# Five of seven down products of a ConvFFN from scaled pairs of float16 instead of pairs of fp32r

## The chip, the core and the metric

The kernel runs on one core of a Trainium2 chip. The metric is the device time of one execution in microseconds (us), the median of several runs. A core has TensorE (PE in the profile, with its weight loads as PEld), VectorE (DVE), ScalarE (ACT), GpSimd (POOL) and SyncE (SP), which here only starts DMAs. Each engine works through its own queue in order, and waits on semaphores of the others.

## The reference

One decoder layer: attention and a gated short convolution side by side, then a feed-forward part with a causal depthwise convolution over time. All of it is float32. What the change touches is the last part:

```python
h2 = rmsnorm(x, norm2_g) * (1 + sc2) + sh2
u = causal_dwconv(h2 @ w_up, ffn_conv_w)          # 3 taps
u_gate, u_val = jnp.split(u, 2, axis=-1)
y = (silu(u_gate) * u_val) @ w_down
return x + g2 * y
```

x is 2048 x 1024, w_up 1024 x 5632, w_down 2816 x 1024.

## The kernel before

The program is one long sequence of stages: modulation and the value projection, the projections of queries and keys, the convolution channels, attention with the output projection behind it, and then the feed-forward part in two halves of 1,024 rows (`hv` 0 and 1). Each half is `up(hv)` and then `down(hv, side)`. Almost all instructions of these stages are pinned in the order in which the Python code issues them (`K` is `tc.keep_in_program_order`), so the code's order is each engine's queue.

**How a float32 product is made.** An operand is split into a high part and the rest, `hi` and `lo`, and the product is three matmuls, hi x hi, hi x lo and lo x hi, into one PSUM accumulator. In `up` the pairs are float16, scaled by powers of two so that they fit float16's range. The scales come from sums of magnitudes: ScalarE's Abs with an accumulator gives a sum per partition, VectorE takes the largest, PE transposes and spreads it. In `down` the pairs are fp32r (float32 that PE reads at reduced precision) and need no scale.

**Seven products for eight.** Both matrix products use a scheme of seven block products in place of eight, with sums and differences of blocks as operands. In `up` the operands are made from the normalized rows (`b11`, `b21`, `t1` to `t4`, `b22`) and from w_up. In `down` they are made from y: `down_inputs` writes seven tensors `y_op` of 512 columns to DRAM. The sums of blocks of w_down (`w_sc`) are written to DRAM much earlier, in the stage of the convolution channels, by `down_sums`: a generator which takes a step after each projection of 512 columns; it loads two rows of blocks of w_down (tiles `wd`, four buffers), makes four sums on VectorE and stores them.

**up(hv).** 22 iterations, one for each 128 columns of the gate half and of the value half. An iteration has seven products of 12 matmuls into three accumulators X, Y and Z, in this order: X, Y, X, Z, Y, Z, Y. Between them stand evictions. ScalarE copies X to `p1` (L1654) before PE adds to X again; VectorE adds `p1` and Y to `u2` and `u3` (L1439) before PE adds to Y again. Each half column then gets three taps: the first on ScalarE (`tap`, L1612), the other two on VectorE (`taps`, L1617). The work on the value half, Silu (L1626), the product y (L1630) and `down_inputs` of iteration i are done in iteration i+1, by the generator `finish`. In half 0 the iteration also prepares the weights of the next one (`up_weights`): ScalarE scales two raw tiles (L1459) and makes the high parts (L1257), VectorE makes block sums (L1439, L1440) and the low parts (L1260); the pairs are stored to DRAM, and half 1 loads them back. Temporaries come from a ring of seven buffers (`t2`).

**down(hv, side).** 77 steps (p, j): seven products p, for each 11 blocks j of 256 rows. The loop variable `e` counts the steps from 0. A step multiplies item e for four tiles of rows: 4 x 3 = 12 matmuls (L1781). Block 9 of each product is done together with block 10, with 24 matmuls, so the step of block 9 has none. An item is a raw tile of 128 x 1024, half from y and half from w_down, loaded six steps ahead by SP's queue. It is split three steps ahead: ScalarE writes `hi` (L1527) and VectorE `lo` (L1528), each one instruction of 1,024 columns; both have four buffers. After block 10 of a product four accumulators are evicted. In each step `side` is also advanced: in half 0 it is the end of `up`, then the late norm of the rows of half 1 (`norm2_late`, twice, with transpositions on PE and many sums on VectorE), in half 1 only the end of `up`.

The step that splits an item is this, and `rim2` below was a small tile that was reserved and not used:

```python
def split_pair(raw):
    hi, lo = pair_tiles()
    K(A.activation(hi, raw, AF.Copy))
    K(V.tensor_tensor(lo, raw, hi.bitcast(F32), op=ALU.subtract))
    y, wd = halves((hi, lo))
    return (*y, *wd)
```

Of the kernel before, what the change touches and what calls it, by code (L numbers as in the profile page):

```python
# [9 lines left out]
F32 = mybir.dt.float32  # L10
# [10 lines left out]
P = 128  # L21
S = 2048
D = 1024
# [23 lines left out]
def kernel(  # L47
# [104 lines left out]
    with ExitStack() as ph:  # L152
# [588 lines left out]
        def down_sums():  # L741

            todo = []

            def load(j):
                ab = [lp.tile([P, D], F32, tag="wd", name="wd", bufs=4) for _ in range(2)]
                for e, w in enumerate(ab):
                    K(nc.sync.dma_start(w, w_down[(2 * j + e) * P : (2 * j + e + 1) * P, :]))
                todo.append(ab)

            def keep(j, n, src0, src1, op):
                t = lp.tile([P, 512], F32, tag="ws", name="ws", bufs=6)
                K(V.tensor_tensor(t, src0, src1, op=op))
                kept.append(lambda: K(nc.sync.dma_start(w_sc[j][:, n * 512 : (n + 1) * 512], t)))
                return t

            kept = []
            load(0)
            yield
            for j in range(NJ):  # L760
                if j + 1 < NJ:
                    load(j + 1)
                while kept:
                    kept.pop(0)()
                (a11, a21), (a12, a22) = [[w[:, 0:512], w[:, 512:1024]] for w in todo.pop(0)]
                s1 = keep(j, 0, a21, a22, ALU.add)
                yield
                keep(j, 2, a11, a21, ALU.subtract)
                s2 = keep(j, 1, s1, a11, ALU.subtract)
                yield  # L770
                keep(j, 3, a12, s2, ALU.subtract)
                yield
            while True:
                while kept:
                    kept.pop(0)()
                yield
# [466 lines left out]
    with ExitStack() as ph:  # L1243
# [27 lines left out]
        def columns(Q, k):  # L1271
# [4 lines left out]
            K(A.activation(h, pt, AF.Identity, bias=sh2[:, k : k + 1], scale=a2[:, k : k + 1]))  # L1276
            return h

        def norm2(Q):

            if Q == 0:
                fp.tile([P, 96], F32, name="rim2")
            ss = fp.tile([P, 16], F32, tag="ss", name="ss", bufs=2)[:, 0:4]
            xn[Q] = kept[Q]
            for t in range(4):
# [239 lines left out]
        def split_pair(raw):  # L1525
# [3 lines left out]
            y, wd = halves((hi, lo))  # L1529
            return (*y, *wd)  # L1530

        plan = (("a11", "b11"), ("a12", "b21"), ("s2", "t2"), ("s3", "t3"), ("a22", "t4"), ("s1", "t1"), ("s4", "b22"))

        def load_operands(hv, p, j):
# [58 lines left out]
        def up(hv):  # L1593
# [25 lines left out]
            def finish(i, p1, Y, gate, val, yg):  # L1619

                taps(yg, gate, i)
                add(val[:, 2:514], p1, Y)
                yield
                yv = tap(val, NPAIR + i)
                keep_halo(val, NPAIR + i)
                K(A.activation(yg, yg, AF.Silu))  # L1626
                taps(yv, val, NPAIR + i)
                yield
                y = fq.tile([P, 1024], F32, tag="hi", name="y", bufs=4)
                K(V.tensor_tensor(y, yg, yv, op=ALU.mult))  # L1630
                down_inputs(i, hv, y)
                yield

            wts, ops = ready.pop("wts"), ready.pop("ops")
            last = None
            for i in range(NPAIR):
# [45 lines left out]
                yg = tap(gate, i)  # L1682
                keep_halo(gate, i)
                next(wts)
                product(Y, o22, "t4", False)
                last = finish(i, p1, Y, gate, val, yg)
            return last

        def down(hv, side):
# [17 lines left out]
                ]  # L1707

            later, spare = [], []

            def rest():
                if not spare:
# [4 lines left out]
            def gated(g, total, n):  # L1717
                K(V.tensor_tensor(g, total, gate[n], op=ALU.mult))
# [5 lines left out]
            def evict(p, t):  # L1724
                a = acc[t]
                if p == 0:
                    K(A.activation(u2[t], a, AF.Copy))
                elif p in (1, 6):
                    g = rest()
                    gated(g, a, 0)  # L1730
                    later.append(lambda: put_out(p == 6, 0, t, g))
                elif p == 2:
                    add(u2[t], u2[t], a)
                elif p == 3:
                    add(u3[t], u2[t], a)
                elif p == 4:
                    g = rest()
                    add(g, u2[t], a)
                    later.append(lambda: gated(g, g, 1))
                    later.append(lambda: put_out(0, 1, t, g))  # L1740
                elif p == 5:
                    add(u3[t], u3[t], a)
                    later.append(lambda: gated(u3[t], u3[t], 1))
                    later.append(lambda: put_out(1, 1, t, u3[t]))
                    later.append(lambda: gated(u2[t], u2[t], 0))
# [5 lines left out]
            for e, (p, j) in enumerate(todo):  # L1751
                while split < min(e + 3, len(todo)):
                    if loaded == split:
                        raws[todo[loaded]] = load_operands(hv, *todo[loaded])
                        loaded += 1
                    pairs[todo[split]] = split_pair(raws.pop(todo[split]))
                    split += 1
                while loaded < min(e + 6, len(todo)):
                    raws[todo[loaded]] = load_operands(hv, *todo[loaded])
# [2 lines left out]
                    flush()  # L1762
                if (p, j) in extra:
                    x1_tiles(*extra[p, j])
                if (p, j) == (6, 5):
                    for t in range(4):
                        with_x1(t)
# [60 lines left out]
```

## Time and profile before

| | us |
|---|---|
| median of 3 runs (lowest, highest) | 2358.12 (2355.66, 2358.35) |
| the profiled execution | 2358.7 |
| its span in the profile | 2357.0 |
| convolution channels, from 360 to 606 | 246.0 |
| up, half 0, from 1118.4 to 1520.8 | 402.4 |
| down, half 0, to 1744.0 | 223.2 |
| up, half 1, to 2142.9 | 398.9 |
| down, half 1, to the end | 214.1 |

The mean granted clock of TensorE was 0.996 of full speed. In a row of the order of time, the first number is the start in us from the start of the span, the second the busy time, then engine, line, operation, `out<-in`, shape, and how many instructions were merged; a bracket at the end gives the idle time of the engine just before and what ended it. Matmuls overlap in the pipeline, so a single one shows about 0.38 us, and the rate is read from the distance of many. In a row of groups, the two numbers after the bar are the busy time in us and the mean of one in ns, then the idle time before them. Names of buffers are shortened: `t` is a tile of the ring `t2`, `w` one of the wide ring `w4` (the gate and value halves with their taps).

### The profile page before, as it was taken

What the parts mean: (1) busy time and instruction counts of PE and PEld (TensorE: products, weight loads), DVE (VectorE), ACT (ScalarE), POOL (GpSimd) and SP (SyncE); (2) the same over time, 40 slices, a digit from 0 to 9 for tenths busy, and PEclk for the clock granted to TensorE, in tenths of its full rate; (3) what the DMA queues carried; (4) which work ended last, traced back from release to release, by engine and by line L of the source; (5) the groups of instructions that cost most, each with busy time, mean ns of one, the idle gap of its engine ahead of it and who ended that gap; (6) DMA issues with size and microseconds to landing.
All of it is one profiled execution on the core that took longest, in us unless ns stands there. A gap on an engine that the chain in (4) does not pass through costs nothing.

```text
span 2357.0 us, 38562 instructions
## 1 busy us (share of the span) xinstructions
PE 2273.1 (96%) x14208; PEld 1357.6 (58%) x14208; DVE 1740.0 (74%) x3412; ACT 1163.1 (49%) x1990; POOL 339.3 (14%) x282
## 2 busy tenths in 40 slices
PE   5899999999899898999999999999999999999999
PEld 5765554444577676444444444578764444446887
DVE  6768895773899898456899999966966565656556
ACT  5745453321688897344555565465522223224333
POOL 0211111111677785001000000000000000000000
PEclk9999999999999999999999999999999999999999
DMA  9346599973799997534456655577664444445766
GB/s 283 135 152 184 153 261 286 301 245 90 147 181 183 214 178 154 190 107 159 155 196 217 218 204 208 210 261 240 215 227 139 161 157 147 152 160 190 232 211 220
DMA packets 452646, 455.25 MB, mean 193 GB/s; under 512 B 191248, under 2 KB 301160, under 8 KB 451432
## 3 DMA queue, kind: packets, MB, share of 16 engines
q1 hardware_dynamic: 445336, 435.94, 62.3%
q10 hardware_dynamic: 4752, 8.46, 1.0%
q0 software_dynamic: 2368, 8.39, 0.9%
q8 instruction: 111, 1.82, 0.3%
q14 instruction: 79, 0.65, 0.1%
HBM read 284.84 MB, written 134.28 MB: 178 GB/s over the span
## 4 chain that ended last, share of the span: by engine, by line
PE 79%; DVE 11%; ACT 4%; DMA 3%; issue 2%; SPq 1%; POOL 0%; DVEq 0%; ACTq 0%
PE acc L1604 28%; PE acc L1781 15%; PE acc L145 13%; PE pr L145 11%; PE pv L145 2%; DVE s_t L1070 2%; PE pt L1107 2%; PE ps L1046 1%; DVE near L1114 1%; PE ps L1047 1%; DMA far<-wide 1%; ACT s_t L1087 1%; PE po L1143 1%; DVE t L1439 1%; PE po L1145 1%
## 5 line engine op out<-in xcount | busy, mean ns | idle before, releaser
L1604 PEld LDWEIGHTS <-pair 128*128 128x128 f16 x3696 | 361.5, 98 | 439.7 <-issue 4.9
L1604 PE MATMUL acc<-t,pair 128*128 128x512 f16 x2112 | 477.4, 379 | 1.9 <-DVE t L1439 1.9
L1604 PE MATMUL acc<-b,pair 128*128 128x512 f16 x1584 | 363.4, 379 | 0.0
L1617 DVE SCALAR_TENSOR_TENSOR w<-w,fcw,w 128x1024 f32<-128x1024 f32 x176 | 226.1, 1285 | 79.4 <-ACT w L1612 73.2
L1528 DVE TENSOR_TENSOR lo<-raw,hi 128x1024 fp32r<-128x1024 f32 x154 | 187.3, 1222 | 117.5 <-ACT hi L1527 109.5
L1527 ACT ACTIVATE hi<-raw 128x1024 fp32r<-128x1024 f32 x154 | 161.0, 1057 | 173.0 <-PE acc L1781 106.8
L1781 PE MATMUL acc<-lo,hi 128*128 128x512 f32 x616 | 240.3, 390 | 3.1 <-DVE lo L1528 3.0
L1781 PE MATMUL acc<-hi 128*128 128x512 f32 x616 | 241.9, 393 | 0.9 <-ACT hi L1527 0.9
L1781 PE MATMUL acc<-hi,lo 128*128 128x512 f32 x616 | 240.1, 390 | 0.0
L145 PEld LDWEIGHTS <-h 128*128 128x128 f16 x1344 | 130.3, 98 | 97.4 <-DVE h L358 5.3
L1612 ACT ACTIVATE w<-w,fcw 128x1024 f32<-128x1024 f32 x88 | 100.6, 1143 | 160.7 <-DVE w L1439 160.7
L145 PE MATMUL acc<-wp,mp 128*128 128x512 f16 x768 | 171.1, 382 | 1.1 <-DVE raw L999 1.0
L1087 ACT ACTIVATE s_t<-s_t,nb,cst 128x2048 f32<-128x2048 f32 (+15 forms) x128 | 164.7, 1288 | 4.8
L1099 POOL TENSOR_TENSOR wide<-s_t,wide 128x1024 f16<-128x1024 f32 x64 | 136.7, 2135 | 5.3
L1781 PEld LDWEIGHTS acc<-lo,hi 128*128 128x128 f32 x616 | 115.7, 188 | 28.5 <-DVE lo L1528 5.1
L1070 DVE CUSTOM_DVE_ANT_0 s_t<-ps,nf,mx 128x512 f32<-128x512 f32 (+1 forms) x192 | 119.5, 643 | 16.5 <-PE ps L1049 8.2
L1781 PEld LDWEIGHTS acc<-hi 128*128 128x128 f32 x616 | 115.6, 188 | 25.1 <-ACT hi L1527 1.3
L1781 PEld LDWEIGHTS acc<-hi,lo 128*128 128x128 f32 x616 | 115.6, 188 | 24.3
L145 PEld LDWEIGHTS <-mp 128*128 128x128 f16 x768 | 75.3, 98 | 88.9 <-issue 3.5
L145 PE MATMUL pr<-h,wh 128*128 128x512 f16 x576 | 126.5, 379 | 0.0
L145 PE MATMUL pr<-h,wl 128*128 128x512 f16 x576 | 125.8, 379 | 0.0
L1046 PE MATMUL ps<-kh,qs 128*128 128x512 f16 (+1 forms) x320 | 110.4, 349 | 13.0 <-DVE mx L1070 11.3
(363 smaller groups left out, 4093.0 us busy)
## 6 DMA issues: line engine op xcount, KB each, us to landing
up_sc<-pair SPq DMA_DIRECT2D x132, 256.0 KB, 2.7
pair<-up_sc SPq DMA_DIRECT2D x132, 256.0 KB, 3.3
wx<-in_w_up_dram SPq DMA_DIRECT2D x88, 256.0 KB, 3.6
raw<-in_w_up_dram SPq DMA_DIRECT2D x44, 512.0 KB, 3.8
y_t<-t SPq DMA_DIRECT2D x88, 256.0 KB, 2.6
raw<-y_t SPq DMA_DIRECT2D x88, 256.0 KB, 3.4
raw<-w_sc SPq DMA_DIRECT2D x88, 256.0 KB, 4.2
y_b<-y SPq DMA_DIRECT2D x66, 256.0 KB, 2.0
```

The costliest lines, as they stand in the source:

```text
L145: ins = T.matmul(acc, lhsT=a, rhs=b, start=st, stop=sp)
L1046: K(T.matmul(ps[:, 0:cw], lhsT=qt, rhs=kh[:, c0 : c0 + cw], start=True, stop=False))
L1070: K(V.tensor_tensor_reduce(out=s_t[:, o0 + c0 : o0 + c0 + cw], in0=ps[:, 0:cw], in1=nf[:, c0 : c0 + cw], scale=1.0, scalar=-3.0e38 if g == ...
L1087: K(A.activation(cols, cols, AF.Exp, bias=nb[:, p : p + 1], scale=qk[:, 4:5], accum_out=un["l"][:, p : p + 1]))
L1099: K(G.tensor_tensor(wide[:, 1, :], s_t[:, WB * P : WU], wide[:, 0, :], op=ALU.subtract))
L1107: K(T.transpose(pt[:, b * P : (b + 1) * P], s_t[:, (b0 + b) * P : (b0 + b + 1) * P], ident))
L1527: K(A.activation(hi, raw, AF.Copy))
L1528: K(V.tensor_tensor(lo, raw, hi.bitcast(F32), op=ALU.subtract))
L1604: K(T.matmul(acc, lhsT=a, rhs=b, start=st, stop=sp, skip_group_check=True))
L1612: K(A.activation(y, u[:, 0:1024], AF.Copy, scale=fcw[:, ct : ct + 1]))
L1617: K(V.scalar_tensor_tensor(y, u[:, m : m + 1024], fcw[:, m * 44 + ct : m * 44 + ct + 1], y, op0=ALU.mult, op1=ALU.add))
L1781: K(T.matmul(acc[t], lhsT=a[:, c], rhs=b, start=st, stop=sp, skip_group_check=True))
```

## The change

Products p = 2 to 6 of `down` take their operands from pairs of float16 that are scaled; p = 0 and 1 stay fp32r. What that needs:

- `down_sums` takes the sum of magnitudes of each of the 22 tiles of w_down (ScalarE, 128 x 1024), and VectorE reduces the 22 columns at the end.
- `up` takes the sum of magnitudes of y of the iteration before (ScalarE, 128 x 1024), in both halves; the last one is taken in `down`, at step 5. The unused output goes to a tile of the ring `t2`.
- `operand_scales`, advanced once a step from step 5 of `down`, makes the two scales and the inverse of their product: a reduction at step 7, a transposition on PE at step 8, a reduction at step 9, a matmul on PE at step 10, small VectorE operations at steps 11 and 12.
- `split_scaled` writes `hi` and `lo` in halves of 512 columns, since y and w_down have different scales: two ScalarE and two VectorE instructions a pair in place of one each.
- the evictions of p = 2 to 6 multiply by the inverse.

```diff
+            ws = bp.tile([P, 2 * NJ], F32, name="wsum", bufs=1)
+            junk = bp.tile([P, D], BF16, name="junk", bufs=1)
...
                 keep(j, 3, a12, s2, ALU.subtract)
-                yield
+                for e in range(2):
+                    w = wide.pop(0)
+                    K(A.activation(junk, w, AF.Abs, accum_out=ws[:, 2 * j + e : 2 * j + e + 1]))
+                yield
+            K(V.tensor_reduce(bf_b[:, 0:1], ws, axis=AX.X, op=ALU.max))
...
+        def sum_of(i, y):
+            junk = fp.tile([P, D], BF16, tag="t2", name="junk", bufs=NTEMP)
+            K(A.activation(junk, y, AF.Abs, accum_out=part["rim"][:, i : i + 1]))
+
+        def operand_scales():
+            rim = part["rim"]
+            m, gm, top, sc, inv = rim[:, 24:26], rim[0:2, 28:30], rim[0:2, 32:33], rim[:, 36:38], rim[:, 40:41]
+            sum_of(NPAIR - 1, part["y"])
+            yield
+            yield
+            K(V.tensor_reduce(m[:, 0:1], rim[:, 0:NPAIR], axis=AX.X, op=ALU.max))
+            K(V.tensor_copy(m[:, 1:2], bf_b[:, 0:1]))
+            yield
+            pt = ps_n.tile([P, 512], F32, tag="n", name="pt")
+            K(T.transpose(pt[0:2, 0:P], m, ident))
+            yield
+            K(V.tensor_reduce(top, pt[0:2, 0:P], axis=AX.X, op=ALU.max))
+            K(V.tensor_scalar(gm, ident[0:2, 0:2], top, None, op0=ALU.mult))
+            yield
+            pt = ps_n.tile([P, 512], F32, tag="n", name="pt")
+            K(T.matmul(pt[:, 0:2], lhsT=ones[0:2, :], rhs=gm, start=True, stop=True))
+            yield
...
+        def split_scaled(raw):
+            hi, lo = [fq.tile([P, 2048], F16, tag=t, name=t, bufs=4)[:, 0:1024] for t in ("hi", "lo")]
+            sc = part["rim"][:, 36:38]
+            for n, (h, r) in enumerate(zip(halves((hi,)), halves((raw,)))):
+                K(A.activation(h[0], r[0], AF.Copy, scale=sc[:, n : n + 1]))
+            y, wd = halves((hi, lo))
+            for n, (h, l) in enumerate((y, wd)):
+                r = raw[:, n * 512 : (n + 1) * 512]
+                K(V.scalar_tensor_tensor(l, r, sc[:, n : n + 1], h, op0=ALU.mult, op1=ALU.subtract))
+            return (*y, *wd)
...
                 next(wts)
+                if i:
+                    sum_of(i - 1, part["y"])
                 product(Y, o22, "t4", False)
...
-                    add(u2[t], u2[t], a)
+                    plus(u2[t], a, u2[t])
...
-                    pairs[todo[split]] = split_pair(raws.pop(todo[split]))
+                    pairs[todo[split]] = (split_pair if todo[split][0] < 2 else split_scaled)(raws.pop(todo[split]))
...
+                if e >= 5:
+                    next(operands, None)
```

Where the order moves, first ScalarE in an iteration of `up` in half 0, before. `pair` is a part of a weight pair, `t` on L1654 is `p1`, and the two instructions on L1612 are the first taps of the gate half and of the value half:

```order
L1674 ACTIVATE t_17254<-acc 128x512
L1257 ACTIVATE pair<-raw 128x1024
L1612 ACTIVATE w_17285<-w_17187,fcw 128x1024
L1608 ACTIVATE halo<-w_17187 128x2
L1257 ACTIVATE pair<-raw 128x1024
L1459 ACTIVATE raw<-raw,cst 128x1024 x2
L1654 ACTIVATE t_17339<-acc 128x512
L1612 ACTIVATE w_17341<-w_17188,fcw 128x1024
```

And the same place of the change, where L1291 is the sum of y:

```order
L1730 ACTIVATE t_17141<-acc 128x512
L1264 ACTIVATE pair<-raw 128x1024
L1667 ACTIVATE w_17172<-w_17077,fcw 128x1024
L1663 ACTIVATE halo<-w_17077 128x2
L1291 ACTIVATE junk,rim_14269<-y 128x1024
L1264 ACTIVATE pair<-raw 128x1024
L1503 ACTIVATE raw<-raw,cst 128x1024 x2
L1710 ACTIVATE t_17226<-acc 128x512
L1667 ACTIVATE w_17228<-w_17078,fcw 128x1024
```

The sum stands after the first tap of the gate half and ahead of the last high part, the scaling of the next raw weights, the copy of X and the first tap of the value half.

Then VectorE at the start of `down` in half 0, before. The row of eight is `lo` of items 5 to 12, and `ss` begins the late norm:

```order
L1630 TENSOR_TENSOR y<-w_18699,w_18770 128x1024
L1440 TENSOR_TENSOR t_18625<-y,t_18625 128x512
L1440 TENSOR_TENSOR t_18797<-y 128x512
L1440 TENSOR_TENSOR t_18797<-y,t_18625 128x512
L1528 TENSOR_TENSOR lo<-raw,hi 128x1024 x8
L1359 TENSOR_SCALAR ss<-ss 128x4
```

And the same place of the change, where `rim` is the tile of the scales:

```order
L1484 TENSOR_TENSOR t_18864<-y,t_18690 128x512
L1572 TENSOR_TENSOR lo<-raw,hi 128x1024 x5
L1300 TENSOR_REDUCE rim_14269<-rim_14269 128x1
L1301 COPY rim_14269<-bf_b 128x1
L1572 TENSOR_TENSOR lo<-raw,hi 128x1024 x2
L1306 TENSOR_REDUCE rim_14269<-pt 2x1
L1307 TENSOR_SCALAR rim_14269<-ident,rim_14269 2x2
L1572 TENSOR_TENSOR lo<-raw,hi 128x1024
L1403 TENSOR_SCALAR ss<-ss 128x4
```

The reduction of the sums stands behind `lo` of item 9, and the one of the transposed sums behind `lo` of item 11. On PE the transposition (L1304) stands ahead of the 12 matmuls of step 8, and the matmul that spreads the result (L1310) behind them, ahead of the 24 of step 10.

More of the change, by code (lines that the diff above doesn't have):

```diff
@@ L764, in down_sums @@
                     kept.pop(0)()
-                (a11, a21), (a12, a22) = [[w[:, 0:512], w[:, 512:1024]] for w in todo.pop(0)]
+                wide = todo.pop(0)
+                (a11, a21), (a12, a22) = [[w[:, 0:512], w[:, 512:1024]] for w in wide]
                 s1 = keep(j, 0, a21, a22, ALU.add)
@@ L1277, in columns @@
             return h
+        part = {}
+        def sum_of(i, y):
[19 more added lines that the diff above has]
+            yield
+            bits = sc.bitcast(I32)
+            K(V.tensor_scalar(sc, pt[:, 0:2], 2.0**-40, 2.0**60, op0=ALU.max, op1=ALU.min))
+            K(V.tensor_scalar(bits, bits, 0x7F800000, None, op0=ALU.bitwise_and))
+            K(V.reciprocal(sc, sc))
+            yield
+            K(V.tensor_scalar(bits, bits, 0x7F800000, None, op0=ALU.bitwise_and))
+            K(V.tensor_scalar(sc, sc, 4096.0, None, op0=ALU.mult))
+            K(V.tensor_tensor(inv, sc[:, 0:1], sc[:, 1:2], op=ALU.mult))
+            K(V.reciprocal(inv, inv))
+            yield
         def norm2(Q):
             if Q == 0:
-                fp.tile([P, 96], F32, name="rim2")
+                part["rim"] = fp.tile([P, 96], F32, name="rim2")
             ss = fp.tile([P, 16], F32, tag="ss", name="ss", bufs=2)[:, 0:4]
@@ L1631, in finish @@
                 down_inputs(i, hv, y)
+                part["y"] = y
                 yield
@@ L1709, in down, with plus @@
             later, spare = [], []
+            inv = part["rim"][:, 40:41]
+            operands = operand_scales()
+            def plus(o, a, b):
+                K(V.scalar_tensor_tensor(o, a, inv, b, op0=ALU.mult, op1=ALU.add))
             def rest():
@@ L1729, in evict @@
                     g = rest()
-                    gated(g, a, 0)
+                    if p == 1:
+                        gated(g, a, 0)
+                    else:
+                        K(V.scalar_tensor_tensor(g, a, inv, gate[0], op0=ALU.mult, op1=ALU.mult))
                     later.append(lambda: put_out(p == 6, 0, t, g))
                 elif p == 2:
-                    add(u2[t], u2[t], a)
+                    plus(u2[t], a, u2[t])
                 elif p == 3:
-                    add(u3[t], u2[t], a)
+                    plus(u3[t], a, u2[t])
                 elif p == 4:
                     g = rest()
-                    add(g, u2[t], a)
+                    plus(g, a, u2[t])
                     later.append(lambda: gated(g, g, 1))
@@ L1741, in evict @@
                 elif p == 5:
-                    add(u3[t], u3[t], a)
+                    plus(u3[t], a, u3[t])
                     later.append(lambda: gated(u3[t], u3[t], 1))
```

## Prediction

> **What bounds the kernel now.** I read the page's busy line first, then the busy time of each engine in stretches, then the chain that ended last, and then the order of time in the places that the change touches.
>
> ```profile
> span 2357.0 us, 38562 instructions
> PE 2273.1 (96%) x14208; PEld 1357.6 (58%) x14208; DVE 1740.0 (74%) x3412; ACT 1163.1 (49%) x1990; POOL 339.3 (14%) x282
> ```
>
> TensorE is busy 96% of the span, so a change pays only through the rate of the products or through what keeps them waiting. In the stretches below the columns are the stretch, its length, then busy us of PE, PEld, DVE, ACT and POOL, the granted clock, and DMA. They are the convolution channels, up of half 0, down of half 0, up of half 1 and down of half 1.
>
> ```profile
> 360.00:606.00 246.00, 242.73 (x1144) 113.14 (x1143) 152.66 (x322) 68.41 (x154) 32.83 (x33) 1.00 0.70 221
> 1118.40:1520.80 402.40, 400.52 (x1850) 180.92 (x1848) 373.26 (x429) 231.98 (x345) 0.90 (x2) 1.00 0.57 201
> 1520.80:1744.00 223.20, 219.20 (x989) 179.05 (x988) 169.86 (x223) 116.47 (x141) 0.00 (x0) 1.00 0.73 241
> 1744.00:2142.90 398.90, 398.90 (x1849) 181.01 (x1848) 235.08 (x262) 113.20 (x177) 0.00 (x0) 1.00 0.48 155
> 2142.90:2357.00 214.10, 209.43 (x924) 173.05 (x922) 132.10 (x139) 81.80 (x80) 0.00 (x0) 1.00 0.67 219
> ```
>
> PE fills every stretch, but up of half 0 is special: VectorE is busy 373.26 of 402.40 us (93%) there, against 235.08 of 398.90 in half 1. The 3.5 us by which half 0 is longer are where VectorE is late:
>
> ```profile
> PE acc L1604 <- DVE t L1439: 1.9, 10, 0.2
> ```
>
> So PE waited for VectorE in 10 of 22 iterations: VectorE sets the pace there together with PE. The chain gives the rates of both kinds of product when nothing is in the way (start, length, count):
>
> ```profile
> 1743.99 398.88 PE acc L1604 x1848
> 2142.87 205.40 PE acc L1781 x906
> ```
>
> A float16 product takes 398.88/1848 = 0.2158 us, an fp32r product of down 205.40/906 = 0.2267 us. The difference is 0.0109 us, 5%.
>
> **The change, term 1: the products.** Five of seven down products are 5 x 132 = 660 matmuls in each half. At the rate of up they take 660 x 0.0109 = 7.2 us less: -7.2 in each half, if nothing else is late. The bound on the other side is no gain (0), if the tiles of down ran at the old rate; I take 7.2, because the row of 1848 has the same shape, type and a weight load before each matmul. [...]
>
> **Term 2: ScalarE's sums of y in up of half 0.** Each iteration but the first gets an Abs over 128x1024 with an accumulator. The nearest row is the square with an accumulator in the norm:
>
> ```profile
> 1546.89 1.06 ACT L1357 ACTIVATE junk<-w 128x1024 bf16<-128x1024 f32 x1
> 1547.86 0.19 ACT L1357 ACTIVATION_READ_ACCUMULATOR junk<-w 128x1 f32 x1
> ```
>
> Its read starts 0.97 us after it and takes 0.19: between 0.97 and 1.16 us of ScalarE; I take the middle, 1.06. ScalarE is busy only 232 of 402 us there, but what matters is where the sum stands. This is ScalarE in one iteration:
>
> ```profile
> 1281.68 1.15 ACT L1612 ACTIVATE w<-w,fcw 128x1024 f32<-128x1024 f32 x1 [1.60 <-DVE w L1439]
> ...
> 1282.83 1.04 ACT L1257 ACTIVATE pair<-raw 128x1024 f16<-128x1024 f32 x1
> 1283.77 2.17 ACT L1459 ACTIVATE raw<-raw,cst 128x1024 f32<-128x1024 f32 x2
> 1285.85 0.57 ACT L1654 ACTIVATE t<-acc 128x512 f32<-128x512 f32 x1
> 1286.33 1.14 ACT L1612 ACTIVATE w<-w,fcw 128x1024 f32<-128x1024 f32 x1
> ```
>
> and VectorE beside it, with the same place of the iteration before, PE's wait and PE's next group on X:
>
> ```profile
> 1268.81 2.60 DVE L1617 SCALAR_TENSOR_TENSOR w<-w,fcw,w 128x1024 f32<-128x1024 f32 x2 [0.54 <-ACT w L1612]
> ...
> 1280.90 0.68 DVE L1439 TENSOR_TENSOR w<-t,acc 128x512 f32<-128x512 f32 x1
> ...
> 1285.98 1.22 DVE L1260 TENSOR_TENSOR pair<-raw,pair 128x1024 f16<-128x1024 f32 x1
> 1287.49 1.28 DVE L1617 SCALAR_TENSOR_TENSOR w<-w,fcw,w 128x1024 f32<-128x1024 f32 x1 [0.30 <-ACT w L1612]
> 1280.24 2.75 PE L1604 MATMUL acc<-t,pair 128*128 128x512 f16 x12 [0.19 <-DVE t L1439]
> ...
> 1288.01 2.75 PE L1604 MATMUL acc<-b,pair 128*128 128x512 f16 x12
> ```
>
> VectorE adds the gate half (1280.90). ScalarE then runs without a gap: first tap of the gate half, halo, high part of a weight pair, two scalings, copy of X, first tap of the value half (1286.33). VectorE needs that last one for its two value taps (1287.49), and it already waits for it, 0.54 and 0.30 us in the two iterations. The sum is put between halo and high part, inside this closed loop. So VectorE's wait grows by the sum's length, unless VectorE has slack behind it. It has little: it is what PE waits for in every second iteration. In the other one it is just on time, so I take 0.15 us off on the mean: 0.9 us for each of 21 sums, +18.9 us. Bounds: 0.6 us each if the wait is partly made up elsewhere (+12.6), 1.16 us each if nothing is (+24.4).
>
> In half 1 the same sums cost nothing: VectorE has no weights to split, and ScalarE waits for PE before the copy of X,
>
> ```profile
> 1964.19 0.60 ACT L1654 ACTIVATE t<-acc 128x512 f32<-128x512 f32 x1 [3.25 <-PE acc L1604]
> ```
>
> and 3.25 us of waiting cover 1.06. The 22 sums of w_down in the convolution stretch are 23 us on a ScalarE that is busy 68.41 of 246 us, and its PSUM tiles come six deep: 0, at most 1 if that cover fails. The later release of the `wd` tiles makes SP's queue wait for ScalarE instead of VectorE; what is queued behind it is loaded some groups ahead, so 0 as well.
>
> **Term 3: the scale chain in down.** At step 7 (counting from 0) VectorE reduces the sums, at step 8 PE transposes them, at step 9 VectorE reduces that, and at step 10 PE spreads the result. Both PE instructions stand in PE's queue ahead of the products of their step, and both wait for VectorE instructions that are queued behind `lo` of a later item: of item 9 for step 8, of item 11 for step 10. Here PE is made to need an item earlier than before. In half 0 items come late from DMA there:
>
> ```profile
> 1545.59 0.39 PE L1781 MATMUL acc<-hi,lo 128*128 128x512 f32 x1
> 1546.83 0.50 PE L1781 MATMUL acc<-hi 128*128 128x512 f32 x1 [0.85 <-ACT hi L1527]
> 1548.09 0.50 PE L1781 MATMUL acc<-lo,hi 128*128 128x512 f32 x1 [0.76 <-DVE lo L1528]
> 1549.31 1.22 DVE L1528 TENSOR_TENSOR lo<-raw,hi 128x1024 fp32r<-128x1024 f32 x1 [1.28 <-ACT hi L1527]
> L928 DVE TENSOR_REDUCE rim<-pt x1: 279/279/279, 913.6 to 913.6; 2x1 f32<-2x128 f32 x1
> ```
>
> Step 10 (24 products, since item 9's are done there) began at 1545.1, two products before the first row, and waited about 2 us for item 10; its last 20 products begin with the third row, so it ended at 1548.1 + 20 x 0.2267 = 1552.6. `lo` of item 11 ends at 1550.5. With a reduce of 0.28 and a small operation of about 0.2, PE starts step 10 at about 1551.2 and ends 24 x 0.2267 = 5.4 later, at 1556.6: +4.0 us (0 if the loads come 4 us earlier, 6 if later). In half 1 the loads are less crowded:
>
> ```profile
> 2162.50 2.52 DVE L1528 TENSOR_TENSOR lo<-raw,hi 128x1024 fp32r<-128x1024 f32 x2 [1.97 <-DMA y_t<-t]
> 2166.09 3.81 DVE L1528 TENSOR_TENSOR lo<-raw,hi 128x1024 fp32r<-128x1024 f32 x3 [1.07 <-ACT hi L1527]
> ```
>
> The second of the last three is item 11; it ends near 2168.5, the chain's two operations near 2169, and PE would have begun step 10, after 108 products, at 2142.9 + 107 x 0.2267 = 2167.2 (the chain's row begins with the second product): +1.8 us (0 to 2.5).
>
> **Term 4: the split in halves.** A scaled pair takes two ScalarE and two VectorE operations of 512 columns instead of one of 1,024 each.
>
> ```profile
> L1528 DVE TENSOR_TENSOR lo<-raw,hi 128x1024 fp32r<-128x1024 f32 x154 | 187.3, 1222 | 117.5 <-ACT hi L1527 109.5 <-PE acc L1781 3.9 <-DMA y_t<-t 3.9
> L1527 ACT ACTIVATE hi<-raw 128x1024 fp32r<-128x1024 f32 x154 | 161.0, 1057 | 173.0 <-PE acc L1781 106.8 <-DMA raw<-w_sc 27.4 <-DVE u L1439 18.0
> L951 ACT ACTIVATE mp<-src,rim x32: 704/707/723, 925.8 to 1085.0; 128x512 f16<-128x512 f32 x32
> 955.64 1.41 DVE L952 SCALAR_TENSOR_TENSOR wp<-wo,rim,wp 128x512 f16<-128x512 f32 x2
> ```
>
> ScalarE: at most 2 x 0.707 - 1.057 = 0.36 us more a pair, beside idle time. VectorE: two such operations end to end took 1.41, against 1.22: 0.19 us more a pair, on 55 pairs a half. In half 1 VectorE has 82 us idle: 0. In half 0 one place has no cover, the end of the late norm of the next rows:
>
> ```profile
> 1678.24 1.23 DVE L1528 TENSOR_TENSOR lo<-raw,hi 128x1024 fp32r<-128x1024 f32 x1 [0.43 <-ACT hi L1527]
> ...
> 1707.37 3.49 DVE L1528 TENSOR_TENSOR lo<-raw,hi 128x1024 fp32r<-128x1024 f32 x3
> 1690.00:1709.00 19.00, 16.91 (x73) 13.02 (x72) 18.93 (x26) 9.85 (x13) 0.00 (x0) 1.00 0.86 259
> ```
>
> From 1678.24, where VectorE waited the last time, to 1707.37 it never rests; 12 `lo` lie there, PE's lead runs out, and PE loses 2.1 us. Twelve pairs add 12 x 0.19 = 2.3. PE would run these 10.5 items 10.5 x 12 x 0.0109 = 1.4 faster and so waits that much more, and the pairs just before add about 0.4: +4.1 us (2 to 6). Evictions become three-operand operations; four a product, behind PE's lead: 0.
>
> **The sum.** Up of half 0: +18.9. Down of half 0: -7.2 + 4.0 + 4.1 = +0.9. Down of half 1: -7.2 + 1.8 = -5.4. Together +14.4. The profiled execution took 2358.7 us (span 2357.0 and 1.7 around it) and would take 2373.1; it lies 0.6 above the median of 2358.1, so I predict 2372.5.
>
> **The rivals.** *The sums are hidden, and it becomes faster* (0.07): VectorE's 29 us of idle time in up of half 0 would hold 21 x 1.06 = 22.3 us. Against it: that idle time lies in short gaps between dependent operations, and the wait that grows ends last. It decides when a sum costs PE less than 0.2 us; 21 x 0.2 would be eaten by term 1. With the loads of step 10 in time in half 0 as well, -14.4 + 4.1 + 1.8 = -8.5: 2349.6. *The sums are hidden but the chain and the split take the gain* (0.08): 0.9 - 5.4 = -4.5, 2353.6, at the edge of what can be told from no change. *The sum also holds up PE directly* (0.10): the copy of X comes 1.06 us later, and PE needs it before it adds to X again. The copy ended at 1286.4 and PE's next group on X began at 1288.0, so 1.6 us are left and 0.5 would remain; if instead a further 0.5 us an iteration were lost, 21 x 0.5 = +10: 2383. *Down's products don't run faster* (0.04): term 1 goes, +14.4: 2387. For it speaks only that fp32r and float16 differ by no more than 5%. *Down's products run faster than up's* (0.01): down would be bound by VectorE, at best 214.1 - 132.1 = 82 us less in half 1: under 2300. [...]
>
> **How the numbers follow.** My forecast has 0.70: 2372.5. With every term at its low bound (12.6, -7.2 + 0 + 2, -7.2) it is 2358.3, with every one at its high bound (24.4, -7.2 + 6 + 6, -7.2 + 2.5) 2382.6. The range 2362 to 2382 takes in all but the low corner, and leaves out the fast rivals and part of the slow ones, 2 in 10. A measurement here can tell about 0.2%, 4.7 us. Slower by more: forecast, direct hold-up and no faster products, 0.84. Faster by more: 0.07, with the first rival and the last, less a part that ends inside. Same: 0.09.
>
> **What would show it.** In the profile after: up of half 0 at about 421 us, with VectorE's L1672 waiting about 1.4 us for ScalarE's L1667 in each iteration and PE waiting for L1483; up of half 1 at 399; PE's transposition L1304 and L1310 with waits before them, 4 us in half 0 and 2 in half 1; down's f16 products 0.216 apart; PE waiting for `lo` in the late norm, 6 us. An up of half 0 under 408 us would prove the main term wrong; a down of half 0 under 219 the smaller ones.

## The result, and the profile after

| | before | change |
|---|---|---|
| median of six runs each, us (lowest, highest) | 2356.89 (2351.88, 2360.85) | 2375.08 (2372.70, 2377.08) |
| ratio (95% interval) | | 1.0070 (1.0058 to 1.0083) |
| the profiled execution, and its span | 2358.7, 2357.0 | 2373.1, 2371.3 |
| ahead of up | 1118.3 | 1119.4 |
| up, half 0 | 402.1 | 417.9 |
| down, half 0 | 223.4 | 223.8 |
| up, half 1 | 398.7 | 398.7 |
| down, half 1, to the end | 214.5 | 211.6 |

The change is slower by 0.7%. The ratios here and below are taken from the fast runs alone, which leaves out one execution of 2422 us of e1_moved_sum and one of 6268 us of e4_constants; the two medians in this table by themselves would give 1.0077. A stage here begins with its first product on PE, so the columns of before differ by a few tenths from those quoted above. The loss lies in up of half 0, +15.8 us; of the gain of the faster products only 2.9 us show, in down of half 1. Between two executions the times ahead of up differ by some us (1115.5 to 1124.7 in the table below) with no change to the order of PE's work there; that part is left out of what follows.

The busy line of the page, and then the same stretches as before (convolution channels, up 0, down 0, up 1, down 1), with the busy us of PE, PEld, DVE, ACT and POOL, the clock and DMA:

```profile
PE 2258.9 (95%) x14214; PEld 1238.7 (52%) x14214; DVE 1765.6 (74%) x3545; ACT 1263.1 (53%) x2232; POOL 339.5 (14%) x282
```

```profile
360.00:606.00 246.00, 242.72 (x1146) 113.43 (x1144) 152.98 (x324) 89.68 (x194) 33.26 (x33) 1.00 0.70 221
1119.40:1537.30 417.90, 401.72 (x1849) 180.48 (x1848) 372.13 (x429) 253.85 (x386) 1.07 (x2) 1.00 0.55 193
1537.30:1761.10 223.80, 211.65 (x994) 121.55 (x993) 182.23 (x289) 132.71 (x200) 0.00 (x0) 1.00 0.73 240
1761.10:2159.80 398.70, 398.70 (x1850) 180.78 (x1848) 235.29 (x262) 134.38 (x218) 0.00 (x0) 1.00 0.48 155
2159.80:2371.30 211.50, 203.66 (x929) 114.10 (x927) 145.29 (x205) 99.05 (x139) 0.00 (x0) 1.00 0.67 222
```

In up of half 0 VectorE does the same work as before (372.13 us) in more time, and ScalarE has 22 us more, which is not much of 417.9. Neither engine is full; what has grown is waiting. The waits in up of half 0, by who waits for whom (total us, times, longest), VectorE's before (PE's is in the prediction):

```profile
DVE w L1617 <- ACT w L1612: 9.9, 21, 1.3
```

and both in the change:

```profile
DVE w L1672 <- ACT w L1667: 27.2, 21, 1.3
...
PE acc L1659 <- DVE t L1483: 16.2, 19, 1.4
```

VectorE waits for a first tap 21 times, 1.3 us each (9.9 us in all before), and PE 16.2 us for VectorE where it lost 1.9 before. The chain of waits runs through the new instruction. One iteration of it, as start, length and what, without the shortest pieces:

```profile
1249.59 0.69 DVE w L1483
...
1250.36 1.15 ACT w L1667
...
1251.61 1.04 ACT junk L1291 x2
1252.64 0.95 ACT pair L1264
1253.59 2.08 ACT raw L1503 x2
1255.67 0.48 ACT t L1710
1256.15 1.05 ACT w L1667
...
1257.22 1.30 DVE w L1672
```

This is the closed loop of the prediction, read from the addition of the gate half on VectorE (1249.59) to the two taps of the value half (1257.22): everything between is ScalarE's, end to end, and `junk` (L1291) is the sum of y, 1.04 us of it.

In down, PE's waits in half 0 before, and then those of the change:

```profile
PE acc L1781 <- DVE lo L1528: 3.0, 4, 1.7
PE acc L1781 <- ACT hi L1527: 0.9, 1, 0.9
```

```profile
PE acc L1849 <- DVE lo L1584: 8.1, 6, 3.0
PE pt L1310 <- DVE rim L1307: 3.0, 1, 3.0
PE pt L1304 <- DVE rim L1301: 1.0, 1, 1.0
```

The two instructions of the scale chain in each half, from PE's order of time:

```profile
1560.46 0.27 PE L1304 MATMUL pt<-ident,rim 128*2 128x128 f32 x1 [0.99 <-DVE rim L1301]
1566.52 0.38 PE L1310 MATMUL pt<-rim,ones 2*128 2x2 f32 x2 [3.05 <-DVE rim L1307]
...
2182.10 0.27 PE L1304 MATMUL pt<-ident,rim 128*2 128x128 f32 x1 [0.23 <-DVE rim L1301]
2187.57 0.38 PE L1310 MATMUL pt<-rim,ones 2*128 2x2 f32 x2 [2.47 <-DVE rim L1307]
```

PE waits 4.0 us for the chain in half 0 and 2.7 in half 1, and 8.1 us for late `lo` (3.9 for `lo` and `hi` together before). All of the 8.1 is for scaled items, from 1701 us on. Of the 3.9 before, 1.6 stood at step 10 (the rows of 0.85 and 0.76 in the prediction); these waits are gone, because the chain's now stand there. A stretch of the chain of waits with nothing late gives the rate of the new products:

```profile
1621.74 33.67 PE acc L1849 x156
```

33.67/156 = 0.2158 us a float16 product, as in up.

### The profile page after: what moved, and what is told of

Read it like the earlier page. It is cut to its first block, busy times and chain, and to the rows that moved or that the text cites. A ratio compares the mean times of both kernels' runs of the same rounds, so it can differ in the third digit from the quotient of the medians.

```text
span 2371.3 us, 38967 instructions
## 1 busy us (share of the span) xinstructions
PE 2258.9 (95%) x14214; PEld 1238.7 (52%) x14214; DVE 1765.6 (74%) x3545; ACT 1263.1 (53%) x2232; POOL 339.5 (14%) x282
## 4 chain that ended last, share of the span: by engine, by line
PE 67%; DVE 15%; ACT 9%; DMA 5%; issue 4%; SPq 1%; POOL 0%; DVEq 0%; ACTq 0%
PE acc L1659 19%; PE acc L145 13%; PE acc L1849 12%; PE pr L145 11%; PE pv L145 2%; ACT w L1667 2%; ACT raw L1503 2%; PE pt L1114 2%; DVE s_t L1077 2%; DVE t L1483 2%; PE ps L1053 1%; DVE near L1121 1%; PE ps L1054 1%; DMA far<-wide 1%; DMA up_sc<-pair 1%
## 5 line engine op out<-in xcount | busy, mean ns | idle before, releaser
L1659 PE MATMUL acc<-t,pair 128*128 128x512 f16 x2112 | 477.3, 379 | 16.2 <-DVE t L1483 16.2
L1849 PE MATMUL acc<-lo,hi 128*128 128x512 f16 (+1 forms) x616 | 235.3, 382 | 8.3 <-DVE lo L1584 8.1
L1849 PE MATMUL acc<-hi 128*128 128x512 f16 (+1 forms) x616 | 236.5, 384 | 0.0
L1849 PE MATMUL acc<-hi,lo 128*128 128x512 f16 (+1 forms) x616 | 235.3, 382 | 0.0
L1580 ACT ACTIVATE hi<-raw,rim 128x512 f16<-128x512 f32 x220 | 145.2, 712 | 102.8 <-PE acc L1849 78.3
L1584 DVE SCALAR_TENSOR_TENSOR lo<-raw,rim,hi 128x512 f16<-128x512 f32 x220 | 154.5, 747 | 51.4 <-ACT hi L1580 51.0
L1849 PEld LDWEIGHTS <-hi 128*128 128x128 f16 x880 | 86.0, 98 | 101.2 <-issue 0.3
L1483 DVE TENSOR_TENSOR t<-t,acc 128x512 f32<-128x512 f32 x88 | 60.1, 683 | 75.2 <-PE acc L1659 75.2
L1264 ACT ACTIVATE pair<-raw 128x1024 f16<-128x1024 f32 x66 | 69.1, 1048 | 85.6 <-DVE raw L1484 85.6
```

What stands on the lines that cost most here:

```text
L1483: add = lambda o, a, b: K(V.tensor_tensor(o, a, b, op=ALU.add))
L1580: K(A.activation(h[0], r[0], AF.Copy, scale=sc[:, n : n + 1]))
L1584: K(V.scalar_tensor_tensor(l, r, sc[:, n : n + 1], h, op0=ALU.mult, op1=ALU.subtract))
L1659: K(T.matmul(acc, lhsT=a, rhs=b, start=st, stop=sp, skip_group_check=True))
L1849: K(T.matmul(acc[t], lhsT=a[:, c], rhs=b, start=st, stop=sp, skip_group_check=True))
```

## The experiments

The theory was the prediction's: the sum of y costs because of where it stands in ScalarE's queue, the scale chain costs because PE meets it before VectorE's results are there, and the float16 products themselves gain about what their rate says. The rivals were that the sum costs as ScalarE's time wherever it stands, and that scaling as such (split in halves, three-operand evictions) eats the gain. Each ratio is to runs of the kernel before on the same chip. Since e5 to e8 ran on another chip than e1 to e4, and e9 and e10 on a third, experiments are compared through these ratios, which tell a difference of about 0.2%, and stage by stage through the profiles, of which there is one for each kernel.

| run | ratio to before (95%) | ahead of up | up 0 | down 0 | up 1 | down 1 | span |
|---|---|---|---|---|---|---|---|
| the change | 1.0070 (1.0058, 1.0083) | 1119.4 | 417.9 | 223.8 | 398.7 | 211.6 | 2371.3 |
| e1_moved_sum | 0.9994 (0.9982, 1.0006) | 1116.7 | 402.1 | 225.1 | 398.7 | 211.5 | 2354.1 |
| e2_late_chain | 1.0042 (1.0027, 1.0056) | 1121.9 | 417.8 | 222.2 | 398.7 | 209.3 | 2369.8 |
| e3_both | 0.9963 (0.9949, 0.9976) | 1117.9 | 402.2 | 219.7 | 398.7 | 208.7 | 2347.2 |
| e4_constants | 0.9959 (0.9943, 0.9975) | 1118.0 | 402.1 | 221.2 | 398.7 | 207.8 | 2347.7 |
| e5_two_sums | one execution, 2401.4 us | 1124.7 | 440.2 | 225.5 | 398.7 | 210.7 | 2399.7 |
| e6_fp32r_again | 1.0016 (1.0006, 1.0027) | 1116.1 | 402.1 | 225.8 | 398.7 | 215.2 | 2357.9 |
| e7_one_scale | 0.9967 (0.9954, 0.9980) | 1115.5 | 402.2 | 220.2 | 398.7 | 209.5 | 2346.1 |
| e8_gpsimd_gates | 0.9988 (0.9976, 1.0000) | 1118.2 | 402.1 | 223.4 | 398.7 | 208.4 | 2350.8 |
| e9_norm_earlier | 0.9988 (0.9979, 0.9996) | 1118.7 | 402.2 | 223.7 | 398.7 | 209.3 | 2352.6 |
| e10_norm_earliest | 1.0030 (1.0020, 1.0041) | 1121.2 | 402.1 | 236.5 | 398.7 | 208.4 | 2366.8 |

### e1_moved_sum: the same sum at another place

```diff
                 K(A.activation(p5, Z, AF.Copy))
+                if i:
+                    sum_of(i - 1, part["y"])
                 product(Y, os3, "t3", False)
...
                 next(wts)
-                if i:
-                    sum_of(i - 1, part["y"])
                 product(Y, o22, "t4", False)
```

> The sum of y of the iteration before stands behind ScalarE's copy of Z (p5) instead of behind the first tap of the gate half; same instruction, same tile ring, same work. My theory (the place in the closed loop of ScalarE and VectorE costs the time): ScalarE waits 2.5 to 3.5 us for VectorE behind that copy, so the sum is covered, up of half 0 goes from 417.9 back to 402 to 404 us, and the time falls by 14 to 16 us to about 2358 to 2360. Rival (it is ScalarE's load or the extra tile of the ring, wherever it stands): up of half 0 stays at 415 to 420 and the time at 2373.

Up of half 0 is back at 402.1 us with the same 21 sums in it. The waits there, and ScalarE at its new place:

```profile
DVE w L1672 <- ACT w L1667: 9.9, 21, 1.3
...
PE acc L1659 <- DVE t L1483: 1.9, 10, 0.2
```

```profile
1255.19 0.60 ACT L1730 ACTIVATE t<-acc 128x512 f32<-128x512 f32 x1 [0.53 <-PE acc L1659]
1255.68 1.05 ACT L1291 ACTIVATE junk<-y 128x1024 bf16<-128x1024 f32 x1
...
1258.30 1.06 ACT L1264 ACTIVATE pair<-raw 128x1024 f16<-128x1024 f32 x1 [1.48 <-DVE raw L1484]
```

Behind the sum ScalarE still waits 1.48 us for a block sum of VectorE: here the sum lies in idle time, and VectorE's wait is 9.9 us, PE's 1.9, as before the change. By the ratios it is 1.0070 - 0.9994 = 0.0076, 18 us. The rival that the sum costs wherever it stands is out, and with it the tile of the ring, which the sum still takes.

### e2_late_chain and e3_both: the scale chain later

PE's transposition moves from step 8 to step 10, the matmul that spreads the result from step 10 to step 12; the scales are first used in step 20.

```diff
             K(V.tensor_copy(m[:, 1:2], bf_b[:, 0:1]))
             yield
+            yield
+            yield
             pt = ps_n.tile([P, 512], F32, tag="n", name="pt")
             K(T.transpose(pt[0:2, 0:P], m, ident))
-            yield
             K(V.tensor_reduce(top, pt[0:2, 0:P], axis=AX.X, op=ALU.max))
             K(V.tensor_scalar(gm, ident[0:2, 0:2], top, None, op0=ALU.mult))
             yield
+            yield
             pt = ps_n.tile([P, 512], F32, tag="n", name="pt")
             K(T.matmul(pt[:, 0:2], lhsT=ones[0:2, :], rhs=gm, start=True, stop=True))
-            yield
             bits = sc.bitcast(I32)
```

> Only the chain of the scales is moved: transposition on PE and its reduction at step 10, the matmul and the scales at step 12, so that neither PE instruction needs an item earlier than the products of its own step do. My theory: PE's waits before the two instructions (4.0 us in half 0, 2.7 in half 1) go; in half 0 about 1 us of waiting for the late item comes back in their place, so the time falls by 5 to 6 us to about 2368. Rival (those waits only take the place of waits for late loads that PE has anyway): the time falls by under 2 us.

The third kernel has the edits of both.

> Both moves together. My theory: the two costs add up, 2373 - 15 - 5.5 = about 2352 to 2353, 0.15 to 0.25% faster than the kernel before. Rival (the costs overlap): over 2357.

No wait of PE for the chain is left in either. The move is worth 0.0028 to 0.0031 by the ratios (the change against e2, e1 against e3), 7 us. The block products p = 0 and 1 of down, in which the chain stands, took together 67.4 us in half 0 and 63.7 in half 1 in the change, 64.9 and 60.7 in e3_both, and 64.6 and 60.1 before: about 0.9 us of the chain is left in both halves together. The two effects add up: e3_both is faster than the kernel before by 0.37% (0.24 to 0.51%), about 9 us, somewhat more than expected, and faster than the change by 1.1%. It is the version to keep.

### e4_constants: no scales to be found

Here all sums of magnitudes and the scale chain are left out, and constants stand in place of the scales and their inverse.

```diff
-                    K(A.activation(junk, w, AF.Abs, accum_out=ws[:, 2 * j + e : 2 * j + e + 1]))
...
+                K(V.memset(part["rim"][:, 36:37], 0.0625))
+                K(V.memset(part["rim"][:, 37:38], 64.0))
+                K(V.memset(part["rim"][:, 40:41], 0.25))
...
-                if i:
-                    sum_of(i - 1, part["y"])
...
-                if e >= 5:
-                    next(operands, None)
```

> Leaves out every sum of magnitudes and the chain; the scales are constants. What is left of the change are the float16 products, the split in halves and the evictions. My theory: up of half 0 at 402, down of half 0 at 220 to 221 (7.2 less for the products, about 5 more for the late norm), down of half 1 at 207.5, together 2350 to 2352, and not lower than the kernel with both moves by more than 2 us. Rival (float16 products in down gain less than 7.2 us in each half): down of half 1 over 210, time over 2355.

Its ratio, 0.9959, can't be told from that of e3_both, 0.9963. So in e3_both the 66 sums and the chain together cost nothing that these ratios can tell: once it stands at the right places, finding the scales is free to within some us, of which the profiles place the 0.9 us above. The sums of w_down in the convolution channels are hidden too, as far as one profile each can tell: the times ahead of up are 1118.0 without them and 1117.9 with them.

### e5_two_sums: the suspected cost twice

The change with the sum of y written two times, one after the other, at its first place.

```diff
                 if i:
                     sum_of(i - 1, part["y"])
+                    sum_of(i - 1, part["y"])
```

> The change as it is, but each sum of y inside the loop of up is taken twice, in both halves, into the same column. My theory (closed loop of ScalarE and VectorE in half 0, cover by ScalarE's waits in half 1): up of half 0 grows by the full length of the second sum, 21 x 1.06 = 22 us, to about 440; up of half 1 stays at 398.7, because its 3.25 us of waiting cover 2.1; the time is about 2395. Rival (ScalarE's place is covered and only the first sum disturbed something): up of half 0 below 425. A third way (PE's group on X becomes the next thing that waits): over 445.

Up of half 0 took 440.2 us, as expected: the second sum costs (440.2 - 417.9)/21 = 1.06 us each, as much as it occupies ScalarE (1.04 in the chain above), while the first had cost (417.9 - 402.1)/21 = 0.75. So the loop had 0.31 us of slack an iteration, and the first sum used it up. The waits in up of half 0 of e5_two_sums:

```profile
PE acc L1659 <- DVE t L1483: 25.9, 19, 1.9
...
PE acc L1659 <- ACT t L1710: 9.4, 18, 0.5
```

The second row was in none of the others: PE waits 0.5 us in 18 iterations for ScalarE's copy of X. That is the mechanism of the prediction's direct hold-up. It gave the copy 1.6 us to spare; two sums make it 2.1 us later, and the 0.5 us that are lacking fit the row. One sum does not reach that far, and even with two the hold-up adds nothing on top of the sum's length.

### e6_fp32r_again and e7_one_scale: products and split

e6_fp32r_again is e3_both with the scaled pairs in fp32r in place of float16; e7_one_scale is e3_both with one instruction of 1,024 columns for `hi` and one for `lo`.

```diff
-            hi, lo = [fq.tile([P, 2048], F16, tag=t, name=t, bufs=4)[:, 0:1024] for t in ("hi", "lo")]
+            hi, lo = pair_tiles()
...
-                K(V.scalar_tensor_tensor(l, r, sc[:, n : n + 1], h, op0=ALU.mult, op1=ALU.subtract))
+                K(V.scalar_tensor_tensor(l, r, sc[:, n : n + 1], h.bitcast(F32), op0=ALU.mult, op1=ALU.subtract))
```

> The kernel with both moves, but the scaled pairs of products 2 to 6 are fp32r again instead of float16, so the sums, the chain, the split in halves and the evictions stay and only the rate of 1,320 products goes back. My theory (0.0109 us a product where PE is never kept waiting): down of half 1 from 208.7 to 215.5 to 216, down of half 0 from 219.7 to 223 to 226 (there part of the gain had gone into waiting in the late norm), time about 2349.5 + 11 to 13 = 2361. Rival (the rate in down does not depend on the type): within 2 us of 2349.5.

```diff
-            for n, (h, r) in enumerate(zip(halves((hi,)), halves((raw,)))):
-                K(A.activation(h[0], r[0], AF.Copy, scale=sc[:, n : n + 1]))
+            K(A.activation(hi, raw, AF.Copy, scale=sc[:, 0:1]))
+            K(V.scalar_tensor_tensor(lo, raw, sc[:, 0:1], hi, op0=ALU.mult, op1=ALU.subtract))
             y, wd = halves((hi, lo))
-            for n, (h, l) in enumerate((y, wd)):
-                r = raw[:, n * 512 : (n + 1) * 512]
-                K(V.scalar_tensor_tensor(l, r, sc[:, n : n + 1], h, op0=ALU.mult, op1=ALU.subtract))
```

> The kernel with both moves, but hi and lo are one instruction of 1,024 columns each again, with the scale of y for both halves (the inverse is still that of two scales, so the result is scaled wrongly). My theory (the halves cost VectorE about 0.1 to 0.15 us a pair against this form, and that counts only in the late norm): down of half 0 falls by 1 to 2 us to about 218, down of half 1 stays, time 2347.5 to 2348.5. Rival (the halves cost nothing that PE sees): no difference. Other rival (the halves are the whole of the waiting in the late norm): 4 us less.

The float16 products are worth 1.0016 - 0.9963 = 0.0053, 12 us, of the 14.4 that the rates give. The stretches of the chain at the end of the program show the rates themselves, in e6_fp32r_again

```profile
2176.10 172.96 PE acc L1850 x762
```

and in e3_both, where the first 120 of these products, the end of p = 1, are still fp32r:

```profile
2171.92 146.59 PE acc L1850 x672
```

0.2270 us, and 0.2181 as a mix of the two rates. The split in halves can't be told from none: 0.9967 stands against 0.9963, and the intervals overlap. The 1 to 2 us expected are less than the ratios can tell, and they don't show in the profiles either, where down takes 220.2 and 209.5 us against 219.7 and 208.7.

### e8_gpsimd_gates: some of VectorE's work to GpSimd

In e3_both PE still waits for `lo` in the late norm of half 0. Four products by the gate and four additions to x after product 4, eight operations of 0.68 us, were given to GpSimd, which is idle there.

```diff
-                    later.append(lambda: gated(g, g, 1))
-                    later.append(lambda: put_out(0, 1, t, g))
+                    later.append(lambda: gated(g, g, 1, G if hv == 0 else V))
+                    later.append(lambda: put_out(0, 1, t, g, G if hv == 0 else V))
```

> The kernel with both moves, and in half 0 the four multiplications by the gate and the four additions of x that follow product 4 run on GpSimd, which is idle there, instead of VectorE. My theory (in the late norm VectorE alone is what PE waits for): 8 x 0.6 = 4.9 us of VectorE's unbroken stretch go, PE's wait for lo falls from 4.4 to 1 us or less, down of half 0 to about 216.5, time about 2346 to 2347. Rival (VectorE is slowed while GpSimd works, or the late results hold up the loads): no gain or a loss.

This one was a miss, and its recorded rival held: it came out slower than e3_both, down of half 0 at 223.4 in place of 219.7 us. GpSimd at that place in e8_gpsimd_gates:

```profile
1679.35 1.72 POOL L1782 TENSOR_TENSOR g<-g,gates 128x512 f32<-128x512 f32 x1
1681.15 1.59 POOL L1785 TENSOR_TENSOR xs<-xs,g 128x512 f32<-128x512 f32 x1
```

VectorE beside it, and again when GpSimd had ended (1689.4):

```profile
1672.63 0.69 DVE L1267 TENSOR_TENSOR b<-t,b 128x512 f16<-128x512 f32 x1
...
1679.87 1.75 DVE L1274 TENSOR_TENSOR t<-t,t 128x512 f32<-128x512 f32 x1
1681.55 3.42 DVE L1267 TENSOR_TENSOR t<-t,t 128x512 f16<-128x512 f32 x2
1684.89 5.75 DVE L1585 SCALAR_TENSOR_TENSOR lo<-raw,rim,hi 128x512 f16<-128x512 f32 x4
1690.57 0.68 DVE L1274 TENSOR_TENSOR t<-b,t 128x512 f32<-128x512 f16 x1
```

A VectorE operation with two inputs took 1.75 us while GpSimd worked and 0.68 before and behind it. VectorE was busy 184.43 us in the stage with the eight operations gone, 182.05 in e3_both with them: its other operations took 8 x 0.68 + 2.4 = 7.8 us longer to save 5.4, at a place where PE had little lead. PE then waited 7.2 us in one piece. The trace does not show why the two slow each other down. VectorE's four evictions at 1675.88 to 1678.60, which read one input from PSUM, kept their 0.74 us beside GpSimd's first operation, which took 1.27 us there in place of 1.7.

### e9_norm_earlier and e10_norm_earliest: the norm spread out

e3_both with the late norm advanced twice in 8 steps, and in 15.

```diff
                 next(side, None)
+                if hv == 0 and e in range(28, 44, 2):
+                    next(side, None)
```

> This is e3_both with one edit: in down of half 0 the late norm is advanced a second time in each of eight steps (28 to 42, even ones), so that its heavy last part on VectorE begins and ends eight steps earlier, and overlaps less with the gates and additions to x after product 4. Nothing else changes. In e3_both PE waits 4.2 us for lo there (the longest 2.98), and behind that wait 14 products run at half rate (0.427 us apart in place of 0.216), about 3 us more. My theory: those 4.2 us are VectorE's unbroken stretch, and the half rate follows the long wait; with the stretch spread both go or shrink below 2 us. Expected: down of half 0 at 213 to 217 us instead of 219.7, no products at half rate, span 2341 to 2345, 4 us less than e3_both on the median. Rival: the stretch only moves to an earlier place, the wait stays: within 1.5 us of e3_both (2349.5). Second rival: the second rows' loads from x_sc come earlier beside the loads of items, and hi waits for DMA: slower than e3_both by 2 to 5 us.

> The same as e9_norm_earlier with 15 second advances (steps 24 to 52, even ones), so the norm's work is denser in the middle of down of half 0 and ends about 15 steps earlier than in e3_both. My theory: the work of VectorE is then packed into fewer steps than it has room for, and PE's wait for lo comes back in the middle, around 1620 to 1680 us, with half rate behind it if it lasts longer than about 2.5 us: 1 to 5 us slower than e9_norm_earlier. Rival: earlier is simply better, no wait comes back: the same as e9_norm_earlier or 1 us faster.

Both fell short of what was expected. In e9_norm_earlier the long wait for `lo` is gone, and others are in its place, 9.4 us in all against 5.4 in e3_both. PE's waits in down of half 0:

```profile
PE acc L1850 <- DVE u L1773: 2.8, 1, 2.8
PE pt L1384 <- ACT t L1388: 2.0, 1, 2.0
PE acc L1850 <- DVE lo L1585: 2.0, 5, 0.5
PE acc L1850 <- ACT hi L1581: 1.0, 2, 0.7
```

The norm brings its own instructions on PE, the transpositions (L1384), and these stand in PE's queue and wait for ScalarE and VectorE; a denser norm also delays the evictions (L1773), which hold the accumulators. I had counted only VectorE's load. The stage is 4.0 us longer, with 4.0 us more of waiting; that the two agree is chance, since fewer products at half rate (8 in place of 14, see the last section) and more short losses behind waits cancel besides. With 15 steps it is 236.5 us. Of the three paces, the one that the kernel had was the best; what would remove the last 5.4 us of waits stays open.

## Why the prediction held, step by step

It said 2372.5 us for the median, with 2362 to 2382, and slower; measured were 2375.08. For the profiled execution it said 2373.1, and it took 2373.1; but that agreement is luck: up of half 0 came out 3.1 us below its term, down of half 1 2.5 us above, down of half 0 0.5 us below, and 1.1 us came from ahead of up. The change itself was put at +14.4 us; the profiles give 14.3, the ratio 16.5 and the medians 18.2.

- **Term 2, the sums of y, up of half 0: +18.9 forecast, +15.8 in the profile.** The mechanism was right (VectorE's wait, the loop, PE's wait for L1483; e1 and e5 show it). The size was 0.75 us a sum and not 0.9, since the slack in the loop was 0.31 us and not 0.15. VectorE's wait was expected at 1.4 us an iteration and was 1.3. By the ratios (the change against e1, e2 against e3) the place of the sum is worth 18 to 19 us, give or take 4; the profiles place 15.6 to 15.8 of them in up, and that is within these intervals.
- **The parts put at nothing** were nothing: up of half 1 at 398.7 with its 22 sums, the convolution channels with PE at 242.72 us (242.73 before) and ScalarE at 89.68 (68.41).
- **Down of half 0: +0.9 forecast, +0.4 measured.** Its waits grew from 3.9 to 12.1 us, 8.2, where terms 3 and 4 had 4.0 + 4.1, but the split was off, and the agreement is luck. The chain made p = 0 and 1 only 2.8 us longer (67.4 in place of 64.6): its waits took the place of 1.6 us that PE had waited there. From 1701 us on PE waited 8.1 us for `lo`, where 6 were forecast for the late norm. And the float16 products gained more than term 1 says: p = 2 to 4 took 90.3 us in place of 95.2, 1.6 each and not 1.4. Little of that lies behind the norm's groups of transpositions on PE: the distance from the first product to the second fell there from 0.31 to 0.22 us, but that from the start of the group to the first product grew from 0.36 to 0.43; where the rest lies is not shown.
- **Down of half 1: -5.4 forecast, -2.9 measured.** This is the term that was mis-sized. The chain was put at +1.8 (0 to 2.5); the two waits are 0.23 + 2.47, and the two PE instructions themselves, 0.27 and 0.38 us, and the slow starts behind them (0.32 and 0.34 us from the first product to the second in place of 0.2267) had been left out. The block product p = 0 took 33.7 us in place of 30.1, so the chain cost 3.6. The last 0.7 us lie at the end of the program: a matmul of the last step starts 0.3 us late, right when its `lo` is done, and from the start of the last matmul to the end it takes 5.4 us in place of 5.05. The evictions with three operands, which the prediction had put at nothing, stand there: the four multiplications by the gate took 0.74 us each in place of 0.69.
- **Term 1, the products: -14.4 forecast.** The rate is 0.2158 as expected, and e6 gives 12 us for both halves. In half 1 each of p = 2 to 5 took 28.5 us in place of 29.9, which is what the rate says.

Of the rivals, the hidden sums are out by 15.8 us, and the direct hold-up by e5, which shows it only from the second sum on. Nor do down's products run faster than up's: 0.2158 us in both.

## What to carry to other kernels

An instruction is priced by its place: the same 1.06 us on ScalarE cost 0.75 us in a loop of dependent steps between two engines, and nothing at another place of the same iteration, with ScalarE far from full in both. Before adding to such a loop, look for the row where that engine waits longest for the other, and put the work there, into the wait. A small chain over several engines should get more steps where there is room before its result is needed: two steps more took its cost here, in both halves together, from 6.4 us to about 1.

## What the runs showed of the hardware that was not expected

**A long wait of PE can cost again.** PE's order of time in e3_both, at its longest wait, for `lo` in the late norm:

```profile
1687.00 0.38 PE L1850 MATMUL acc<-hi 128*128 128x512 f16 x1
1690.36 0.58 PE L1850 MATMUL acc<-lo,hi 128*128 128x512 f16 x1 [2.98 <-DVE lo L1585]
1690.74 0.63 PE L1850 MATMUL acc<-hi,lo 128*128 128x512 f16 x1
1691.16 0.63 PE L1850 MATMUL acc<-hi 128*128 128x512 f16 x1
...
1696.29 0.41 PE L1850 MATMUL acc<-hi 128*128 128x512 f16 x1
1696.53 0.38 PE L1850 MATMUL acc<-lo,hi 128*128 128x512 f16 x1
```

Ahead of the wait and behind 1696.5 the products are 0.216 us apart. From 1690.36 to 1696.29 there are fourteen, all but the first 0.427 us apart, half the rate, which costs 5.93 - 14 x 0.2158 = 2.9 us on top of the wait. The granted clock from 1690.4 to 1696.4 was 0.51 (0.69 as the mean of 1690.1 to 1700.1). The change had a wait of the same length at the same place, and no slower product behind it; the granted clock from 1710.1 to 1716.1 was 1.00:

```profile
1710.12 0.38 PE L1849 MATMUL acc<-lo,hi 128*128 128x512 f16 x1 [2.98 <-DVE lo L1584]
1710.33 0.38 PE L1849 MATMUL acc<-hi,lo 128*128 128x512 f16 x1
```

From up of half 0 on, the profiles of the change and of the ten experiments have 17 waits of PE over 2 us. Behind 10 of them, all of 2.72 us or more, 7 to 14 products ran at half rate, some at once and some only about 1 to 3.5 us later; 4 others of 2.97 to 3.05 us and the 3 under 2.5 us had none. The kernel before has no wait over 2 us there, and no such products. Why the same 2.98 us are followed by products at half rate in e3_both and by none in the change, no run here shows. So a wait near 3 us should be priced with up to 3 us more (2.9 in e3_both), and two profiles that differ by as much in such a stage tell nothing.

**GpSimd and VectorE side by side** were slower than VectorE alone (e8 above): moving eight operations with two inputs from SBUF off VectorE, which was busy 9.93 of each 10 us from 1670.1 to 1690.1 in e3_both, made down of half 0 3.7 us longer (223.4 in place of 219.7).
